# A hybrid decoder layer: the input projection with tokens kept on chip and weights streamed, in matmuls of 416 columns

## The chip, the cores and the metric

The kernel runs on one core of one Trainium2 chip. The metric is the device time of one launch in microseconds (us). The core has five engines that run side by side: TensorE (PE in the profile; PEld is its weight load), VectorE (DVE), ScalarE (ACT), GpSimd (POOL) and SyncE (SP). Here SyncE issues most transfers (its queue is SPq), GpSimd some stores, ScalarE a few loads. Matmuls read on-chip memory (SBUF) and write to PSUM, eight banks of 512 float32 columns in each of 128 partitions.

## The reference, cut to what matters

One layer for 4096 prompt tokens and 64 sample tokens, 4160 in all, with model width 1024:

```python
h = _rmsnorm(x, g_pre)
z = h @ w_in                      # 1024 -> 2816 columns
cb, cc, ch, cg, q, k, v, ag, mq, mg = _split_cols(z)
u = cc * ch                       # gated convolution over 3 tokens
conv = conv_w[0] * up[:, 0:t] + conv_w[1] * up[:, 1:t + 1] + conv_w[2] * up[:, 2:t + 2]
out_a = jax.nn.silu(cg) * cb * conv
out_b = jax.nn.silu(ag) * o_b     # o_b: attention in a window of 128 keys
out_c = jax.nn.silu(mg) * o_c     # o_c: attention over 256 memory tokens
y = jnp.concatenate([out_a, out_b, out_c], axis=-1) @ w_out
return x + _rmsnorm(y, g_post), new_conv, new_k, new_v
```

The change concerns `z = h @ w_in`: 4160 tokens, 22 column tiles of 128, 1024 values to sum over.

## The kernel before, in words

**Precision.** A float32 number is split into a high part (rounded to the format that TensorE multiplies) and a low part (the rest). A product of two split operands takes three matmuls per 128 values summed over: high x high, high x low, low x high. A split is a copy on ScalarE and a subtraction on VectorE: lines 183 and 187 for weights, 359 and 360 for tokens.

**Seven products for eight.** Two column tiles make a *pair*, two halves of the 1024 inputs make the rows, two half blocks of tokens make the columns: a 2 x 2 by 2 x 2 block product. Strassen's scheme in Winograd's form computes it with seven products in place of eight, from sums S1 to S4 of the weight blocks A11 to A22 and sums T1 to T4 of the token blocks B11 to B22 (`PRODUCTS`, line 40). Each product is four slices of 128 inputs x three matmuls = 12 matmuls (`product`, line 364, the matmul in line 369) of `HW` = 260 columns. `evict` (line 372) adds what a product left in PSUM to z tiles in SBUF: line 376 on VectorE, line 378 on ScalarE.

**Loops.** The 11 pairs are in three phases (`PHASES`, line 43) of 4, 4 and 3 pairs. In a phase the weights stay split on chip, and the eight blocks of 2 x 260 tokens pass by: for each phase, for each block, for each of the seven products, for each pair. Phase 0 scales the tokens by the gain and the row factor, and writes them to DRAM (`hd`), the sums T1 to T4 are written in phase 1, and later phases read them again. The first two blocks of phase 0 multiply plainly (eight products), before row factors are there, and scale z afterwards (`z_rows`, line 621). Sums of weights for a later phase are made during the phase before it and go through DRAM (`w_sums`, line 196).

**Ends.** What a column tile becomes follows in `finish` (line 486): a gate with a tanh (`finish_gate`, lines 429 and 430), a split q or k (`finish_parts`, lines 410 and 412), v (`finish_v`), or the convolution (`finish_conv`). The results go to DRAM (`md`, `qd`, `vd`) and are read by the attention.

**Order.** In phase 0 every engine runs in the order in which the code issues its instructions (`in_order`); in phases 1 and 2 a planner orders them, but for some that are held in program order. Phase 2 also computes keys and values of the memory tokens (`mem_acc`, line 794) and the attention of chunk 0, the first 256 of the prompt tokens. After the projection, `open_attention` (line 1010) opens the attention's buffers; there the 15 other chunks run between the matmuls of the output projection (line 1482).

Of the kernel before, what the change touches and what calls it, by code (L numbers as in the profile page):

```python
# [23 lines left out]
HW = 260  # L24
NBLK = NT // (2 * HW)
# [7 lines left out]

PRODUCTS = (("A11", "B11"), ("A12", "B21"), ("S2", "T2"), ("S3", "T3"), ("S1", "T1"), ("S4", "B22"), ("A22", "T4"))  # L40
NP_ = len(PRODUCTS)

PHASES = (((8, 9), (14, 15), (16, 17), (12, 13)), ((0, 1), (2, 3), (4, 5), (6, 7)), ((10, 11), (18, 19), (20, 21)))
PLAIN_BLOCKS = 2
# [7 lines left out]
def hybrid_layer(ctx: ExitStack, tc: tile.TileContext, a: dict):  # L52
# [6 lines left out]

# [4 lines left out]
    ones = const.tile([P, P], F32, name="ones")  # L64
    G.memset(ones, 1.0)
# [3 lines left out]
    convw = const.tile([P, 2, 3], F32, name="convw")  # L69

    zs = const.tile([P, 14, NS], F32, name="zs")

    diag = const.tile([P, 2 * HW], F32, name="mix_s")
    mix_s = diag[:, : 8 * NS].rearrange("p (k n) -> p k n", n=NS)

    rowd = [tc.dram_tile([2 * HW], F32, name=f"rowd{b}") for b in range(NBLK)]
    hd = [{o: tc.dram_tile([P, KH, HW], F32, name=f"hd{b}_{o}") for o in ("B12", *(o for _, o in PRODUCTS))}
          for b in range(NBLK)]
    sd = {}
    qd = tc.dram_tile([2, 7, P, NT], F32R, name="qd")  # L80
    vd = tc.dram_tile([P, NT], F32, name="vd")
    md = tc.dram_tile([KT, P, NT], F32, name="md")

    wa = ctx.enter_context(tc.tile_pool(name="wa", bufs=3 * NP_))
    pa = ExitStack()
    wb_stack = ExitStack()
    wb = wb_stack.enter_context(tc.tile_pool(name="wb", bufs=NP_, side="right"))  # L90
    psa = ExitStack()

    place = ctx.enter_context(tc.tile_pool(name="place", bufs=1)).tile([P, 2, KH, HW], F32, name="place")
    hxp = pa.enter_context(tc.tile_pool(name="hx", bufs=4))
    hp = pa.enter_context(tc.tile_pool(name="hp", bufs=2))
    own = ExitStack()
    kept_z = ExitStack()
    zp, used = {}, {1: [], 2: []}

    def z_pool(where, name, w=2):  # L100
        return where.enter_context(tc.tile_pool(name=name, bufs=1))

    def open_phase(ph):
        nonlocal tp, natp, pa2, pa1

        if ph == 0:
            z = [z_pool(kept_z, f"z{n}") for n in range(4)]
            natp = own.enter_context(tc.tile_pool(name="nat", bufs=2))
            zp[2] = [*z, z_pool(own, "z4")]
            kept_z.z4 = zp[2][-1]  # L110
        elif ph == 1:
            zp[2].remove(kept_z.z4)
            zp[2][:0] = [z_pool(own, f"z{n}") for n in (5, 6, 7)]
        else:

            tp = [own.enter_context(tc.tile_pool(name=f"t2{n}", bufs=3)) for n in "ab"]
            z = [z_pool(own, n) for n in ("z8", "z9", "y0", "y1", "z10", "y2")]
            zp[2], zp[1] = [z[0], z[1], z[4]], [z[2], z[3], z[5]]
        if ph < 2:
            tp = own.enter_context(tc.tile_pool(name=f"t{ph}", bufs=(7, 9)[ph]))  # L120
        if ph != 1:

            psa.close()
            bank = lambda name, bufs: psa.enter_context(tc.tile_pool(name=name, bufs=bufs, space=bass.MemoryType.PSUM))
            if ph == 0:

                pa2 = {tag: bank(f"pa{tag}", 2) for tag in "xy"}
            else:

                pa1 = {(tag, w): bank(f"p{tag}{w}", 1) for tag, w in (("x", 2), ("x", 1), ("y", 1), ("y", 2))}  # L130
                third["ps"] = bank("psm", 2)

    tp = natp = pa2 = pa1 = None

    def accumulator(i, w, name):
# [20 lines left out]
    def flush():  # L156
        for fn in late:
            fn()
# [1512 lines left out]
```

## Time and profile before

| what | before |
|---|---|
| median of 3 runs | 1543.01 us (1542.81 to 1544.86) |
| the profiled execution: its span from first to last instruction | 1539.4 us |
| granted TensorE clock, mean over the span | 0.999 |
| TensorE matmul, busy | 1529.5 us |
| VectorE, busy | 1146.7 us |
| ScalarE, busy | 806.7 us |
| GpSimd, busy | 380.7 us |
| moved by DMA | 305.59 MB, mean 199 GB/s |

The profiled execution's own launch time isn't listed apart from the runs; its span lies 3.6 us under their median, which is what lies around a span. A row of the windows reads: stretch in us from the span's start, its length, busy us of PE, PEld, DVE, ACT and POOL (each with its count of instructions), granted clock, share of time that the 16 DMA engines were busy, GB/s moved. A row of the chain reads: start, duration, engine, tile and line, count. A row of the timeline reads: start, duration, engine, line, operation, output and inputs with shapes, count, and in brackets the idle time before it with what ended it. A row of the groups reads: line, engine, operation, output and inputs, shapes, count, then busy us, mean ns of one, and the idle time of the engine just before them with what ended most of it. Matmuls are pipelined, so the duration of one matmul (0.28 us) is longer than the distance between two.

### The profile page before, as it was taken

The numbers are of one execution on the slowest core, as the hardware profiler recorded it, in microseconds if no ns is written. First come the engines' busy times: TensorE is split into PE (matmuls) and PEld (weight loads), VectorE is DVE, ScalarE is ACT, GpSimd is POOL, SyncE is SP. The second block draws the span as 40 slices with busy tenths as digits, with TensorE's granted clock in tenths as the row PEclk, the third lists the DMA queues.
The fourth block names the chain that finished last, engine by engine and source line by source line (L and its number), as shares of the span: only waits on it lengthen the run. The fifth ranks groups of instructions, "written<-read, shape, count | busy, mean of one in ns | idle before, by whom it ended". The sixth has DMA issues, their size and how long they took to land.

```text
span 1539.4 us, 30166 instructions
## 1 busy us (share of the span) xinstructions
PE 1529.5 (99%) x11341; PEld 1407.9 (91%) x11341; DVE 1146.7 (74%) x2059; ACT 806.7 (52%) x2047; POOL 380.7 (25%) x603
## 2 busy tenths in 40 slices
PE   9999999999999999999999999999999999999998
PEld 9999999999999999999999998788888888888876
DVE  6789888899888777897777769766666666666643
ACT  6686666476222222354454437765566556555632
POOL 0223332221400000000101203644444444444310
PEclk9999999999999999999999999999999999999999
DMA  9989999878755333677876789977777777777332
GB/s 261 180 239 252 271 272 263 276 241 288 193 180 180 126 126 126 214 223 280 223 258 236 217 295 266 228 165 148 161 148 148 151 156 153 157 160 150 124 110 96
DMA packets 175110, 305.59 MB, mean 199 GB/s; under 512 B 31093, under 2 KB 104821, under 8 KB 174933
## 3 DMA queue, kind: packets, MB, share of 16 engines
q1 hardware_dynamic: 128069, 226.69, 47.5%
q0 software_dynamic: 46176, 75.92, 24.7%
q8 instruction: 90, 1.47, 0.4%
q10 hardware_dynamic: 720, 1.05, 0.2%
q14 instruction: 55, 0.45, 0.1%
HBM read 196.54 MB, written 108.05 MB: 198 GB/s over the span
## 4 chain that ended last, share of the span: by engine, by line
PE 94%; DVE 2%; DMA 1%; ACT 1%; POOL 1%; issue 0%; ACTq 0%; SPq 0%; DVEq 0%; POOLq 0%
PE c L369 55%; PE y L1482 23%; PE ws L1250 4%; PE wo L1092 2%; PE wt L1273 2%; PE xs L1186 2%; PE xt L1201 2%; PE wo L1222 2%; PE wo L1228 1%; PE mem_acc L794 1%; DMA qd<-z 1%; DMA ws20A<-in_w_in 0%; POOL xp L1195 0%; DVE z L376 0%; DVE z L625 0%
## 5 line engine op out<-in xcount | busy, mean ns | idle before, releaser
L1482 PE MATMUL y<-wo,mh 128*128 128x512 f32 (+1 forms) x1040 | 350.1, 399 | 0.0
L376 DVE TENSOR_TENSOR z<-c,z 128x520 f32<-128x520 f32 (+1 forms) x308 | 195.3, 647 | 99.0 <-PE c L369 96.7
L1482 PEld LDWEIGHTS y<-wo,mh 128*128 128x128 f32 x1040 | 194.3, 188 | 39.3 <-issue 2.4
L1482 PE MATMUL y<-wo,ml 128*128 128x512 f32 (+1 forms) x520 | 201.8, 388 | 0.0
L1263 ACT ACTIVATE sm<-sm,wnm 128x128 f32<-128x128 f32 x256 | 99.6, 390 | 61.6 <-DVE wnm L1257 60.3
L1195 POOL TENSOR_SCALAR xp<-xp,xrd 128x256 f32<-128x256 f32 x128 | 76.9, 608 | 200.3 <-DVE xrd L1191 200.1
L1482 PEld LDWEIGHTS y<-wo,ml 128*128 128x128 f32 x520 | 98.2, 189 | 16.2
L1187 DVE TENSOR_REDUCE xmx<-xs 128x2 f32<-128x512 f32 x64 | 44.1, 689 | 58.2 <-PE xs L1186 58.1
L1275 ACT COPY wpt<-wt 128x512 f32<-128x512 f32 x64 | 37.2, 582 | 85.8 <-PE wt L1273 85.7
L1250 PEld LDWEIGHTS ws<-kst,q 128*128 128x128 f32 x512 | 70.0, 190 | 5.2 <-ACT xp L1190 0.5
L1489 DVE TENSOR_TENSOR yn<-y,gpost 128x512 f32<-128x512 f32 (+1 forms) x66 | 45.1, 683 | 39.6 <-PE y L1482 39.3
L1250 PE MATMUL ws<-kst,q 128*128 128x256 f32 x512 | 73.1, 283 | 0.1
L1490 ACT ACTIVATE y<-y 128x512 f32<-128x512 f32 (+1 forms) x66 | 38.6, 584 | 64.5 <-DVE yn L1489 64.5
L742 POOL CAST wmask<-negs 128x256 uint8<-128x256 f32 x1 | 0.8, 841 | 268.5 <-DMA negs<-in_wmask 268.5
L1190 ACT ACTIVATE xp<-xs,xnm 128x256 f32<-128x256 f32 x128 | 58.9, 464 | 7.0 <-DVE xnm L1188 6.7
L1283 POOL TENSOR_SCALAR_AFFINE_SELECT wpt<-wpt 128x512 f32<-128x512 f32 x64 | 51.2, 800 | 43.6 <-ACT wpt L1275 40.6
L1125 POOL DMA_DIRECT2D q<-qd x64 | 42.8, 674 | 71.5 <-DVE wo L187 61.1
L1280 POOL TENSOR_SCALAR_AFFINE_SELECT wpv<-wpt 128x512 f32<-128x512 f32 x62 | 40.4, 652 | 59.7 <-ACT wpt L1275 59.5
L1253 DVE COPY_PREDICATED sm<-wmask,ws 128x256 f32<-128x256 uint8 x124 | 52.2, 436 | 3.0 <-ACT sm L1252 2.8
L1114 POOL DMA_DIRECT2D kst<-qd x64 | 38.6, 617 | 63.8 <-PE xt L1201 41.5
L1500 DVE SCALAR_TENSOR_TENSOR xr<-yn,yst,xr 128x1024 f32<-128x1024 f32 (+2 forms) x34 | 43.1, 1269 | 14.1 <-POOL yst L1496 13.4
L378 ACT COPY z<-c 128x520 f32<-128x520 f32 (+1 forms) x44 | 24.4, 554 | 52.8 <-PE c L369 49.9
(962 smaller groups left out, 5135.6 us busy)
## 6 DMA issues: line engine op xcount, KB each, us to landing
q<-qd POOLq DMA_DIRECT2D x64, 384.0 KB, 8.0
xr<-in_x_p SPq DMA_DIRECT2D x32, 512.0 KB
nat<-in_x_p SPq DMA_DIRECT2D x39, 416.0 KB
o_yp<-xr SPq DMA_DIRECT2D x31, 512.0 KB
md<-th POOLq DMA_DIRECT2D x48, 260.0 KB, 6.4
qd<-zh SPq DMA_DIRECT2D x48, 260.0 KB
qd<-z SPq DMA_DIRECT2D x48, 260.0 KB
kst<-qd POOLq DMA_DIRECT2D x60, 192.0 KB, 5.7
```

Source lines behind the costliest of these rows:

```text
L369: TE.matmul(bank[:, :HW], l, r, start=first and i == 0, stop=last and i == 3 * KH - 1)
L376: add = lambda dst, other: V.tensor_tensor(dst, c, other, op=ALU.add)
L1187: V.tensor_reduce(mx[:, :nb], s, axis=AX.X, op=ALU.max)
L1190: S.activation(p[:, i, :], s[:, i, :], AF.Exp, bias=nm[:, i : i + 1], scale=SCALE, accum_out=den[:, i : i + 1])
L1195: G.tensor_scalar(p[:, i, :], p[:, i, :], rd[:, i : i + 1], 0.5, op0=ALU.mult, op1=ALU.mult)
L1250: TE.matmul(s3[:, hh, :], self.q[:, 4 + 2 * (2 * half + hh) + kvh, i * P : i * P + P], self.kst[:, 2 * kvh + part, i * P : i * P + 2 * P], ...
L1253: V.copy_predicated(sm[:, 2 * half : 2 * half + 2, :], third["wmask"], third["negs"] if first else s3[:, :, 0:P])
L1263: S.activation(sm[:, hh, :], sm[:, hh, :], AF.Exp, bias=nm[:, hh : hh + 1], scale=SCALE, accum_out=den[:, hh : hh + 1])
L1283: G.affine_select(p3, p3, pattern=[[0, 4], [1, P]], compare_op=ALU.is_ge, fill=0.0, base=0, channel_multiplier=-1)
L1482: TE.matmul(acc, self.hl[l][:, k], wo[k][c0 // 512][:, r, c0 % 512 : c0 % 512 + c1 - c0], start=j == 0, stop=j == passes * KT - 1)
L1489: V.tensor_tensor(yn[:m, c0:c1], acc[:m], gpost[:m, c0:c1], op=ALU.mult)
L1500: V.scalar_tensor_tensor(self.xr[:m, cs], yn[:m, cs], st[:m, 3:4], self.xr[:m, cs], op0=ALU.mult, op1=ALU.add)
```

## The change

- `HW` is 416: five blocks of 2 x 416 tokens. A block's seven split token operands lie in seven places in SBUF (`slot`), and the weights of all 11 pairs pass by: for each block, for each of six groups of pairs (five of two pairs, one of one pair), for each product, for each pair of the group. Tokens are read once from the input; `hd` and `sd` are gone.
- In block 0 and in the first group of block 1, weights are loaded raw, summed (S1 and S3 on GpSimd, S2 and S4 on VectorE) and split, and the split sums are stored in DRAM (`wd`). From there on split sums are loaded from `wd`, and A11, A12 and A22 are loaded raw and split again for every block.
- The products come in another order. Products 1 and 3, 2, 4 and 6, and 5 and 7 share a PSUM accumulator each ("AYAYZYZ"): a later product adds to what is there, and each state is read out by one VectorE addition or ScalarE copy.
- Only group 0 of block 0 multiplies plainly. In block 0 all z tiles are scaled by the row factors after the products (`z_rows`); in later blocks the tokens are scaled (`x_scale`).
- Every engine runs in written order to the end of the projection. A step is one product of one group; what happens in which step is set out in `plan_weights`, `plan_tokens`, `plan_ends`, `plan_start` and `plan_third`. In `step`, loads are issued first, then the first pair's product, half of the jobs, the second pair's product, the other jobs, and the eviction.
- Chunk 0 and the memory keys run in the last block. The output weights lie in the token operands' place.

The diff, cut to its core:

```diff
-HW = 260
-NBLK = NT // (2 * HW)
+HW = 416
+BW = 2 * HW
+NBLK = NT // BW
...
-PRODUCTS = (("A11", "B11"), ("A12", "B21"), ("S2", "T2"), ("S3", "T3"), ("S1", "T1"), ("S4", "B22"), ("A22", "T4"))
+PRODUCTS = (("A11", "B11"), ("S2", "T2"), ("A12", "B21"), ("S3", "T3"), ("S1", "T1"), ("A22", "T4"), ("S4", "B22"))
...
-PHASES = (((8, 9), (14, 15), (16, 17), (12, 13)), ((0, 1), (2, 3), (4, 5), (6, 7)), ((10, 11), (18, 19), (20, 21)))
-PLAIN_BLOCKS = 2
+PLAIN = (("A21", "B11"), ("A11", "B11"), ("A21", "B12"), ("A11", "B12"), ("A22", "B21"), ("A12", "B21"), ("A22", "B22"), ("A12", "B22"))
+
+GROUPS = (((14, 15), (16, 17)), ((0, 1), (2, 3)), ((4, 5), (6, 7)), ((18, 19), (20, 21)), ((12, 13),), ((8, 9), (10, 11)))
...
+    x1 = pool(ctx, "x1").tile([P, 6 * XS], F32R, name="x1")
+    x6 = pool(x2, "x2").tile([P, XS], F32R, name="x2")
+    zp = [pool(own, f"z{n}") for n in range(3)]
+    wp = [pool(own, f"w{n}") for n in range(5)]
...
+    wp.append(pool(early, "w5"))
...
+    def load_split(key):
+        b, g, q, o = key
+        w = ws[key] = w_of().tile([P, 2, 512], F32R, tag="w", name="w{}_{}_{}{}".format(*key))
+        DMA.dma_start(f(w), wd[GROUPS[g][q], o])
...
+    def fill_sum(key):
+        b, g, q, o = key
+        w = split_w(key, raws[key] if o == "S2" else raws.pop(key))
+        t = wd[GROUPS[g][q], o] = tc.dram_tile([P, 2, 512], F32, name=f"wd{g}_{q}{o}")
+        store(t, f(w))
+
+    def sums(b, g, q):
+        r = {o: raws.pop((b, g, q, o)) for o in ("A11", "A21", "A22")}
+        G.tensor_tensor(r["A22"], r["A21"], r["A22"], op=ALU.add)
+        G.tensor_tensor(r["A21"], r["A11"], r["A21"], op=ALU.subtract)
+        V.tensor_tensor(r["A11"], r["A22"], r["A11"], op=ALU.subtract)
...
+    def x_scale(b, o):
+        x, half = xs[b, o], int(o[2]) - 1
         for k in range(KH):
+            V.scalar_tensor_tensor(x[:, k], x[:, k], gain_of(o, k), rows[b][:, half * HW : (half + 1) * HW], op0=ALU.mult, op1=ALU.mult)
...
+    def z_rows(b, z):
+        z = z.rearrange("p a b n -> p a (b n)")
+        w = z.shape[1]
+        V.tensor_tensor(z, z, rows[b].unsqueeze(1).to_broadcast([P, w, BW]), op=ALU.mult)
...
+                if b == 0 or (b, g) == (1, 0):
+                    for t, o in ((s0 - 5, "A11"), (s0 - 4, "A21"), (s0 - 3, "A22"), (s0 - 2, "A12")):
+                        load_at(t, lambda o=o, b=b, g=g, qs=qs: [load_raw((b, g, q, o), o) for q in qs])
+                    key = lambda o, b=b, g=g, qs=qs: [(b, g, q, o) for q in qs]
+                    job_at(s0 - 2, *(lambda k=k: split_keep(k) for k in key("A11")))
+                    job_at(s0 - 1, *(lambda b=b, g=g, q=q: sums(b, g, q) for q in qs))
+                    job_at(s0 - 1, *(lambda k=k: fill_sum(k) for k in key("S2")))
+                    job_at(s0, *(lambda k=k: split_keep(k) for k in key("A12")), *(lambda b=b, g=g, q=q: last_sum(b, g, q) for q in qs))
+                    load_at(s0 + 1, lambda b=b, g=g, qs=qs: [load_raw((b, g, q, "A22"), "A22") for q in qs])
+                    job_at(s0 + 1, *(lambda k=k: fill_sum(k) for k in key("S3")))
+                    job_at(s0 + 2, *(lambda k=k: fill_sum(k) for k in key("S1")))
+                    job_at(s0 + 3, *(lambda k=k: fill(k) for k in key("A22")))
+                    job_at(s0 + 4, *(lambda k=k: fill_sum(k) for k in key("S4")))
+                else:
+                    for p, (o, _) in enumerate(PRODUCTS):
+                        u = s0 + p
+                        keys = [(b, g, q, o) for q in qs]
+                        if o[0] == "S":
+                            load_at(u - 2, lambda keys=keys: [load_split(k) for k in keys])
+                        else:
+                            load_at(u - 4, lambda keys=keys, o=o: [load_raw(k, o) for k in keys])
+                            job_at(u - 2, *(lambda k=k: fill(k) for k in keys))
...
+            for i, o in enumerate(("B11", "B12", "B22", "B21")):
+                load_at(s(3, 1 + i), lambda b=b, o=o: x_load(b, o))
+            for t, o in ((s(3, 6), "B11"), (s(4, 1), "B12"), (s(4, 3), "B22"), (s(4, 5), "B21")):
+                job_at(t, lambda b=b, o=o: x_scale(b, o))
+            sums_ = {(5, 0): "T1", (5, 1): "T3", (5, 3): "T2", (5, 5): "T4"}
+            for (g, p), o in sums_.items():
+                job_at(s(g, p), lambda b=b, o=o: x_sum(b, o))
+            for t, o in ((s(5, 2), "B11"), (s(5, 4), "T2"), (s(5, 4), "B21"), (s(5, 6), "T3"),
+                         (at[b, 0, 0], "T1"), (at[b, 0, 1], "T4"), (at[b, 0, 2], "B22")):
+                job_at(t, lambda b=b, o=o: x_split(b, o))
...
+        job_at(5, tsum("T1"))
+        job_at(6, tsum("T3"))
+        job_at(7, tsum("T2"), split("T2"))
+        job_at(8, split("T3"))
+        job_at(9, split("T1"), tsum("T4"))
+        job_at(10, split("T4"))
...
+                elif (b, g) == (0, 0):
+                    front_at(n, *scale(1), *done(1))
+                    front_at(n + 1, *scale(0), *done(0))
+                else:
+                    front_at(n - 1, *scale(1), *done(1))
+                    front_at(n, *scale(0), *done(0))
...
+        jobs = [*first.pop(i, ()), *jobs_at.pop(i, ())]
+        half = (len(jobs) + 1) // 2
...
+            (wo_, xo), c, begin, end = PRODUCTS[p], "AYAYZYZ"[p], p in (0, 1, 4), True
+        if begin:
+            zs_of.setdefault("acc", {})[c] = accumulator(f"c{b}_{g}_{p}")
+        acc = zs_of["acc"][c]
+        for q in qs:
+            product(ws[b, g, q, wo_], slot(3) if plain and xo == "B12" else operand[xo], acc[:, q], begin, end, not (plain or begin))
+            if q == 0:
+                for fn in jobs[:half]:
+                    fn()
...
+        for fn in jobs[half:]:
+            fn()
...
+            evict(p, acc, *zs_of[b, g])
```

In the prediction a group's *first eviction* in a bank that is used again is that of product 2 (S2 x T2), whose accumulator product 4 adds to; a *pair* is one pair of column tiles; *parts* are the splits of q and k.

1021 lines of the change are left out of this document (374 added, 647 removed).

## The prediction

> **What bounds the kernel now.** I read the page first (busy shares), then the table of windows, then the chain that ended last, in order of time.
>
> ```profile
> span 1539.4 us, 30166 instructions
> PE 1529.5 (99%) x11341; PEld 1407.9 (91%) x11341; DVE 1146.7 (74%) x2059; ACT 806.7 (52%) x2047; POOL 380.7 (25%) x603
> ...
> 600.00:640.00 40.00, 40.00 (x336) 40.00 (x336) 30.91 (x42) 12.78 (x17) 0.00 (x0) 1.00 0.43 153
> 690.00:700.00 10.00, 10.00 (x86) 10.00 (x85) 8.08 (x12) 5.80 (x12) 0.00 (x0) 1.00 1.02 354
> ...
> 5.67 0.39 PE L369 MATMUL c<-hi_0B,w_0A 128*128 128x260 f32 x1 [0.25 <-ACT w_0A L183]
> ...
> 112.75 239.31 PE c L369 x1992
> 710.00 1.37 PE mem_acc L794 x6
> 937.44 6.83 PE y L1482 x30
> 1001.50 2.77 PE y L1482 x12
> 1038.27 2.77 PE y L1482 x12
> ```
>
> TensorE is the bound: the chain runs through L369 for 239 us at a stretch, and the granted clock is 1.00. In steady flow 336 matmuls of 260 columns take 40 us, **119 ns** each; a matmul of 512 columns takes 1.37/6 = **228.3 ns**. Busy PE is no measure of waiting, so I count. The projection runs from 5.67 to 937.44 = 931.8 us. It holds (2 plain blocks x 32 + 6 x 28 + 8 x 28 + 8 x 21) products x 12 = 7488 matmuls x 0.119 = 891.1; 48 memory matmuls x 0.2283 = 11.0; and chunk 0 of the attention, 14.9 (a chunk's period, 1038.27 - 1001.50 = 36.8, less its 96 output matmuls x 0.2283). What is left, **14.8 us**, is all that TensorE waits there.
>
> **The change: the matmuls.** After it there are 2 x 8 + (5 x 11 - 2) x 7 = 387 products x 12 = 4644 matmuls of 416 columns. Columns hardly fall: 7488 x 260 = 1.947 million, 4644 x 416 = 1.932. What can be won is the part of a matmul's time that isn't columns. No row has 416: in proportion to 260 it would be 190.4 ns, in proportion to 512 185.5; on the line between the two rows 119 + 156/252 x 109.3 = **186.7**, taken since 416 lies between. 4644 x 0.1867 = 867.0, so -24.1 us (-6.9 to -29.6). [...] A step (one product, two weight pairs, 24 matmuls) becomes 4.48 us, with one pair 2.24.
>
> **VectorE: what it now does, and when.** All five engines' work in the projection is now in written order. In every step the eviction of the product stands behind all the step's other jobs on VectorE, and the product two steps later adds to or overwrites the same PSUM bank: an eviction that is late by over one step stops TensorE.
>
> ```profile
> L376 DVE TENSOR_TENSOR z<-c,z 128x520 f32<-128x520 f32 (+1 forms) x308 | 195.3, 647 | 99.0 <-PE c L369 96.7 <-DMA qd<-zh 1.6
> 13.90 1.68 DVE L590 SCALAR_TENSOR_TENSOR lo_0B<-x_0B,gpre,hi_0B 128x260 fp32r<-128x260 f32 x4
> 15.50 0.69 DVE L187 TENSOR_TENSOR w_0A<-wr_0A,w_0A 128x512 fp32r<-128x512 f32 x1
> 16.10 0.69 DVE L187 TENSOR_TENSOR w_1A<-wr_1A,w_1A 128x512 fp32r<-128x512 f32 x1
> ...
> 101.56 1.23 DVE L349 TENSOR_TENSOR x_2T<-place,x_2B 128x1040 f32<-128x1040 f32 x1
> 102.71 2.39 DVE L625 TENSOR_TENSOR z<-z,rb 128x1040 f32<-128x1040 f32 x2
> ...
> L359 ACT CAST hi_3T<-x_3T 128x1040 fp32r<-128x1040 f32 x8 | 8.5, 1062 | 8.0 <-PE c L369 4.8 <-DMA x_3T<-hd_T 3.2
> L429 ACT ACTIVATE th<-z 128x520 f32<-128x520 f32 x48 | 28.7, 634 | 16.2 <-DMA md<-th 11.8 <-DVE w_2A L187 1.8 <-DVE z L625 1.3
> ```
>
> In a queue a 512-element operation starts 0.60 after the last, one of 1040 1.15 after: 1.04 ns an element and 0.07. So 416 elements cost 0.5, 832 (gate, part, eviction) 0.93, 1664 (an x sum, an x split, a z scaling) 1.8; an x scaling, four of 416, 2.3 (from 1.68 for four of 260). ScalarE: 1.5 for a 1664 cast, 0.9 for 832.
>
> A steady group (blocks 1 to 4) needs 3 x 1.2 weight splits + 5 x 0.9 evictions + some 4 to 6 of gates and parts: under half of its 31.4 us. **Block 0 and the first group of block 1** also do, per group, 4 x 1.2 more splits and 4 x 0.6 of weight sums on VectorE (7.2), and in block 0 two z scalings (3.6), on top of the next block's token work (scalings 9.2, sums 7.2, splits 12.6). I set VectorE's queue against TensorE's steps, place by place, counting from the start of the plain products as if nothing waited there (they end at 8 x 4.48 = 35.8):
> - Group 1. In the last plain step T2's sum, cast and split end at 35.6, since ScalarE's cast stands behind an eviction. Behind them: S2's sums and splits 2.5, a z scaling 1.8, two gates that each wait for a tanh 3.1, T3's split 2.0, A12's splits 1.2, S4's sums 1.2: 47.4. Then a scaling 1.8, gates 3.0, T1's split 2.1, T4's sum 1.8, S3's splits 1.2, and only then the second product's eviction: 58.2. TensorE has done three products by 35.8 + 13.4 = 49.2 and needs that bank: **wait 9**.
> - Groups 2 and 3 (convolution): some 29 of 31.4 us, bunched at the seam: **1.5** together.
> - The last step of group 3 and group 4 (one pair, steps of 2.24). Step 7 of group 3 has 9.0 (eviction, scaling, two parts, sum, split, token scaling, eviction), group 4's steps 4.9, 3.4, 0.6, 3.4, 1.1, 4.0 and 3.8: 30 us of work in 4.5 + 15.7 of TensorE. Waits: 3.4 for S2, behind the parts and GpSimd; 6.2 for A12, behind scaling and parts; 1.9 for the first eviction: **11.5**.
> - Group 5: steps of 6.1, 3.9, 3.0, 3.9, 5.7, 3.9 and 8.8, so 35 in 31.4. Waits: 3.5 for S2, which GpSimd's four sums hold, 3.0 for the first eviction: **6.5**.
> - Seam to block 1: 8.8 and 7.9 in two steps of 4.48, with tanh and GpSimd to wait for: 4.8 for S2, 4.2 for A12, 3.0 for the eviction: **12**.
>
> Together **40**. The floor, where the work alone exceeds TensorE's time, is 2 (group 1: 33 in 31.4) + 10 + 4 = 16.
>
> **GpSimd.** It now makes S1's and S3's sums, 512 elements with two inputs, a form that no row has.
>
> ```profile
> L1283 POOL TENSOR_SCALAR_AFFINE_SELECT wpt<-wpt 128x512 f32<-128x512 f32 x64 | 51.2, 800 | 43.6 <-ACT wpt L1275 40.6
> L458 POOL TENSOR_TENSOR us<-z,z 128x64 f32<-128x64 f32 x2 | 7.1, 3568 | 31.0 <-DVE z L376 31.0
> L483 POOL TENSOR_TENSOR mix_s<-cacc,z 128x64 f32<-128x64 f32 x2 | 0.9, 462 | 0.2
> L1268 DVE TENSOR_TENSOR sm<-sm,wrd 128x512 f32<-128x512 f32 x64 | 44.0, 688 | 1.1
> L165 POOL DMA_DIRECT2D md<-th x48 | 26.2, 547 | 66.6 <-DVE th L430 44.4 <-DVE zs L432 19.1 <-DVE place L349 2.0
> ```
>
> Bounds 0.46 and 3.57; I take 1.0, near the 512-element row. VectorE waits for ten of them in groups 4, 5 and the seam, 10 x (0.46 to 3.57) in place of 10, so the 40 lies between 35 and 66. Stores of stored sums queue on GpSimd too (0.55 each, 8 a group): some 13 of 31 us, no bound.
>
> **Transfers.** Gone: the h blocks' writing and rereading. Added: in blocks 1 to 4 weights stream again, per pair 3 x 0.26 + 4 x 0.52 = 2.9 MB. A block moves 31.7 weights + 6.8 tokens + 9.8 results = 48 MB in 172.5 us, 280 GB/s, against 354 sustained above at no PE wait. Two steps of lead (8.96) cover 1.05 MB at 330 (3.2), what stands ahead on SyncE's queue and a landing; in group 4 the lead is 4.5. Cost 0 to 20, I take **4**.
>
> **Start, steady blocks, end.**
>
> ```profile
> 10.00:20.00 10.00, 10.00 (x84) 10.00 (x85) 7.28 (x13) 6.47 (x13) 0.00 (x0) 1.00 1.02 297
> 160.00:200.00 40.00, 40.00 (x336) 40.00 (x335) 33.25 (x40) 24.37 (x44) 12.66 (x20) 1.00 0.99 277
> 240.00:280.00 40.00, 40.00 (x335) 40.00 (x335) 32.92 (x41) 22.64 (x39) 12.64 (x20) 1.00 0.96 265
> 13.16 1.72 ACT L589 ACTIVATE hi_0B<-x_0B,gpre 128x260 fp32r<-128x260 f32 x4
> ...
> L277 ACT ACTIVATE nat<-nat 104x1024 f32<-104x1024 f32 x40 | 42.1, 1054 | 7.4 <-DMA nat<-in_x_p 7.4
> L277 ACT ACTIVATION_READ_ACCUMULATOR nat<-nat 104x1 f32 x40 | 7.4, 186 | 0.0
> ```
>
> Before step 2, 2.75 MB must land (B11, A21, A11, B12): 9.3 us at 297 from 1 us on, then 2.2 for the gain (four of 260 take 1.72), 1.5 cast, 1.8 split: late by 2 against a step 2 that would start some 9 us after the first matmul at 6. ScalarE's three squares (1.05 + 0.19 each) then wait for four row loads that are queued ahead of A12, so B21's and B22's splits come 2 and 1 late: **5** (0 to 8). Steady group 4 has the token scaling and group 3's parts against steps of 2.24: 2 in each of blocks 1 to 3, **6**. Last block (buffers one fewer, chunk 0's pieces in order on every engine) and the handover, where the last eviction holds the first output product: **3** (0 to 8). From 937 on the work is the same.
>
> **Sum.** Waits 5 + 40 + 6 + 4 + 3 = 58 for 14.8: +43.2; matmuls -24.1; +19.1. The profiled span is 1539.4 us, and the median of the runs 1543.0 has 3.6 around it: **1543.0 + 19.1 = 1562**.
>
> **Rivals.**
> - *Faster: VectorE's queue lags, and TensorE waits only where the work itself is too much.* Place: the seams of block 0; price 16 for the 40, with start 4 and other waits 5: 25, 1543 - 24.1 - 14.8 + 25 = 1529. It decides below 36 of waits in all. For it: before, VectorE is busy 33 of 40 us with all 336 matmuls in place. Against: there VectorE stands idle before evictions for 97 us in all, waiting for TensorE, so they are not queued behind other work as the new ones are.
> - *Transfers bound blocks 1 to 3.* If the mix gets no more than the 265 to 277 GB/s seen at a share near 1.0, a block needs 48.3/0.265 = 182 us for 174.5: +23 for the 4: 1581. Against: 354.
> - *No gain in the matmul.* At 190.4 ns: +17.2, 1579.
> [...]
> - *It moves nothing*: waits of 36 to 42 balance the matmuls: 1543.
>
> **Chances.** Forecast 0.44, faster 0.27, nothing 0.06, transfers 0.11, matmul 0.07, lock 0.05. About 0.2% (3 us) is what can be told from no change: faster 0.27, same 0.06, slower 0.67. The low end, 1532, takes in about half of the faster rival (some 0.13 stays below it); the high end, 1594, takes in the transfers, the matmul and the lock one at a time, and most of GpSimd's upper bound (1562 + 26); some 0.06 stays above, where two of them meet. Cases of one sign hold two thirds, so the likeliest one's own range stands beside it: 1550 to 1575.
>
> **What would show it.** Right: matmul starts 187 ns apart; TensorE gaps on VectorE's evictions and splits between 35 and 260 us, 40 in all; later blocks near 174 us each. Wrong: block 0 without gaps (VectorE queued less than I add up), gaps on weight loads in blocks 1 to 4 (transfers), matmuls 190 apart, or GpSimd sums far from 1.0. The largest risk is the 40: it is added by hand from a queue's order.

## The result and the profile after

| | before | after |
|---|---|---|
| median of 4 runs each, on the same chip | 1543.2 us | 1682.61 us (1677.95 to 1687.96) |
| ratio, 95% interval | | 1.0902 [1.0877, 1.0927] |
| span of the profiled execution | 1539.4 us | 1679.3 us |
| granted TensorE clock, mean over the span | 0.999 | 0.967 |

The forecast was 1562 in a range from 1532 to 1594. The direction came out, the size did not: the loss is 139 us where 19 were forecast.

First the head of the page of the changed kernel, with the slices of TensorE's busy time and of the granted clock:

```profile
span 1679.3 us, 23937 instructions
...
PE 1552.4 (92%) x8489; PEld 1403.4 (84%) x8489; DVE 1012.0 (60%) x1743; ACT 729.4 (43%) x1864; POOL 428.8 (26%) x667
...
PE   8799587997999989998998988799999999999998
...
PEclk9899798999999999998999999899999999999999
```

Before, both were at 9 throughout the projection. Here TensorE has holes, and so has the clock, the deepest of them in the first seven slices (to 294 us), where weights are summed for the first time. The windows put numbers to it. They are cut at the last evictions of block 1's first group (the last one with weight sums), of blocks 1, 2 and 3, and of the projection; the last two rows are stretches of steady flow:

```profile
8.20:300.50 292.30, 235.76 (x1123) 224.17 (x1124) 204.94 (x230) 126.06 (x195) 95.36 (x113) 0.90 0.68 221
300.50:458.00 157.50, 147.65 (x767) 144.11 (x766) 84.98 (x101) 49.09 (x72) 12.61 (x21) 0.99 0.85 262
458.00:643.00 185.00, 177.15 (x928) 174.65 (x928) 103.10 (x119) 62.60 (x87) 15.29 (x26) 0.99 0.85 265
643.00:829.00 186.00, 176.13 (x908) 173.18 (x906) 103.47 (x119) 61.60 (x87) 15.28 (x26) 0.97 0.84 262
829.00:1066.40 237.40, 211.77 (x1086) 198.97 (x1086) 120.12 (x185) 86.72 (x179) 38.94 (x66) 0.94 0.77 230
...
480.00:520.00 40.00, 40.00 (x214) 39.70 (x213) 15.22 (x20) 8.69 (x13) 2.16 (x4) 1.00 0.68 225
302.00:362.00 60.00, 60.00 (x320) 59.53 (x319) 24.38 (x31) 16.71 (x28) 1.62 (x3) 1.00 0.81 240
```

The whole projection before, from its first to its last matmul, in the same view:

```profile
5.67:937.44 931.77, 930.26 (x7667) 922.80 (x7668) 748.79 (x1065) 465.73 (x803) 128.54 (x190) 1.00 0.74 225
```

Length less the PE column is TensorE's idle time: 56.5 us, then 9.9, 7.9 and 9.9, then 25.6, together 110; before, it came to 1.5 us. The clock column adds a second loss: in windows of 1 us, busy time x (1 - granted clock), summed, gives 19.5 us to 300.5, 7.9 in what follows of blocks 1 to 3 and 8.7 in block 4: **36 us** lost while TensorE was busy at half speed; before, 0.0. The rows of steady flow show what went right. A row also counts the matmuls that lie across its edges, and in the difference of two rows they cancel: 320 - 214 = 106 matmuls in 20 us, 188.7 ns each. Before, by the two rows that the prediction shows, it was 336 - 86 = 250 in 30 us, 120.0 ns.

What ended TensorE's waits, up to 1110 us (columns: engine and line, what it waited for, us in total, times, longest):

```profile
PE c L603 <- DMA w_0S<-wd_0S: 28.6, 8, 5.0
PE c L603 <- ACT w_0S L140: 24.2, 4, 14.6
PE c L603 <- ACT z L612: 18.9, 7, 5.0
PE c L603 <- DVE z L610: 18.8, 9, 8.4
PE vtp L903 <- DMA vT<-vd: 9.4, 1, 9.4
```

Three kinds: stored weight sums that land late (w_0S from wd, all behind 370 us), weights that are split late (ACT w_0S, all in block 0 and the first group of block 1), and evictions on ScalarE (L612) and VectorE (L610) that stand behind other work. The longest wait and what follows it, from the timeline of TensorE:

```profile
170.82 2.43 PE L603 MATMUL c<-x,w_0A 128*128 128x416 f32 x12
187.79 4.56 PE L603 MATMUL c<-x,w_0S 128*128 128x416 f32 x12 [14.55 <-ACT w_0S L140]
196.60 3.95 PE L603 MATMUL c<-x,w_0A 128*128 128x416 f32 x12 [4.25 <-ACT z L612]
```

Twelve matmuls take 4.56 us behind the wait, where twelve in flow take 2.43 from first start to last end: half speed. Now what SyncE did ahead of that wait (timeline of SyncE's queue; duration is the time that issuing took):

```profile
155.85 6.01 SPq L189 DMA_DIRECT2D x1B<-in_xt  x2
161.96 1.92 SPq L148 DMA_DIRECT2D wr_0A<-in_w_in  x1
172.40 0.34 SPq L255 DMA_DIRECT2D rb<-rowd  x1
172.79 6.24 SPq L189 DMA_DIRECT2D x1B<-in_xt  x2
179.13 3.23 SPq L148 DMA_DIRECT2D wr_0A<-in_w_in  x3
...
381.95 2.23 SPq L153 DMA_DIRECT2D w_0S<-wd_0S  x1
384.28 0.38 SPq L153 DMA_DIRECT2D w_1S<-wd_1S  x1
394.93 0.32 SPq L255 DMA_DIRECT2D rb<-rowd  x1
395.34 0.94 SPq L189 DMA_DIRECT2D x2B<-in_xt  x2
...
397.31 1.45 SPq L153 DMA_DIRECT2D w_0S<-wd_0S  x2
```

Line 255 spreads the row factors of the next block over the partitions. It stands in SyncE's queue from 163.9 on and is issued at 172.40, and from 384.7 on and is issued at 394.93, since it reads what GpSimd writes, and that write takes long. Behind it stand weights of group 4. Its waits are 29.5 us in blocks 1 to 3:

```profile
SPq L255 <- DMA rowd<-r: 29.5, 3, 10.2
```

The write itself, from the view of the transfers from 150 to 180 us (columns: count, size, us from issue to landing):

```profile
rowd<-r POOLq DMA_DIRECT2D x1, 3.2 KB, 15.4
```

3.2 KB take 15.4 us. The write was issued at 157.0, and it doesn't suffer alone: from some 6 us after its issue all transfers crawl. Block 1's write, issued at 381.3, shows it too (windows of the changed kernel; the last two columns are the DMA engines' busy share and GB/s):

```profile
381.00:386.00 5.00, 5.00 (x29) 4.96 (x28) 1.36 (x2) 0.00 (x0) 1.03 (x2) 1.00 1.08 365
387.00:393.00 6.00, 5.72 (x31) 5.33 (x29) 1.02 (x1) 0.00 (x0) 0.00 (x0) 1.00 1.26 74
```

The engines stay busy and move a fifth. The other three writes behind the start do the same: 411 GB/s from 157 to 162 us and 91 from 164 to 170, 373 and then 118 in block 2, 374 and then 110 in block 3. So the spread isn't the only link between the write and TensorE's waits. The stored sum that TensorE waits for until 397.74 was issued at 381.95, ahead of the spread, and landed some 16 us later:

```profile
397.74 2.76 PE L603 MATMUL c<-x,w_0S 128*128 128x416 f32 x7 [5.02 <-DMA w_0S<-wd_0S]
```

Of the six waits on stored sums in blocks 1 to 3, three (10.8 us) are on such loads, and three (11.6 us) on loads that were issued behind the spread.

### The profile page after: what moved, and what is told of

It reads as the page before. It is cut to its first block, busy times and chain, and to the rows that moved or that the text cites. A ratio compares the mean times of both kernels' runs of the same rounds, so it can differ in the third digit from the quotient of the medians.

```text
span 1679.3 us, 23937 instructions
## 1 busy us (share of the span) xinstructions
PE 1552.4 (92%) x8489; PEld 1403.4 (84%) x8489; DVE 1012.0 (60%) x1743; ACT 729.4 (43%) x1864; POOL 428.8 (26%) x667
## 4 chain that ended last, share of the span: by engine, by line
PE 44%; issue 2%; DMA 2%; DVE 1%; ACT 1%; POOL 0%; SPq 0%; DVEq 0%; POOLq 0%; ACTq 0%
PE y L1235 21%; PE c L603 8%; PE ws L1003 3%; PE wo L845 2%; PE wt L1026 2%; PE xs L939 2%; PE xt L954 2%; PE wo L975 2%; PE wo L981 1%; DMA vT<-vd 1%; PE mem_acc L517 1%; DMA gpost<-in_gpost 0%; DMA kst<-qd 0%; DMA qd<-zh 0%; DVE z L610 0%
## 5 line engine op out<-in xcount | busy, mean ns | idle before, releaser
L603 PE MATMUL c<-x,w_0S 128*128 128x416 f32 x1392 | 303.9, 370 | 73.3 <-DMA w_0S<-wd_0S 28.6
L1235 PE MATMUL y<-x 128*128 128x512 f32 (+1 forms) x1296 | 369.0, 399 | 0.0
L603 PEld LDWEIGHTS c<-x,w_0S 128*128 128x128 f32 x1392 | 274.4, 200 | 87.2 <-ACT w_0S L140 34.7
L1235 PEld LDWEIGHTS y<-x 128*128 128x128 f32 x1296 | 238.2, 189 | 46.1 <-issue 1.6
L603 PE MATMUL c<-x,w_0A 128*128 128x416 f32 x1140 | 241.4, 362 | 26.7 <-ACT z L612 18.9
L603 PEld LDWEIGHTS c<-x,w_0A 128*128 128x128 f32 x1140 | 219.6, 195 | 35.1 <-ACT z L612 21.4
L610 DVE TENSOR_TENSOR z<-c,z 128x832 f32<-128x832 f32 (+1 forms) x145 | 137.2, 946 | 164.7 <-PE c L603 158.9
L603 PE MATMUL c<-x,w_1S 128*128 128x416 f32 x1152 | 236.4, 354 | 0.0
L603 PEld LDWEIGHTS c<-x,w_1S 128*128 128x128 f32 x1152 | 218.8, 191 | 2.8 <-issue 0.4
L603 PE MATMUL c<-x,w_1A 128*128 128x416 f32 x960 | 196.4, 354 | 0.0
L603 PEld LDWEIGHTS c<-x,w_1A 128*128 128x128 f32 x960 | 180.9, 190 | 2.8 <-issue 1.2
```

Source lines behind the costliest of these rows:

```text
L603: TE.matmul(bank[:, :HW], l, r, start=first and i == 0, stop=last and i == 3 * KH - 1, skip_group_check=more)
L610: add = lambda dst, other: V.tensor_tensor(dst, c, other, op=ALU.add)
L1235: TE.matmul(acc, self.hl[l][:, k], wo[k][c0 // 512][:, r, c0 % 512 : c0 % 512 + c1 - c0], start=j == 0, stop=j == passes * KT - 1)
```

## The experiments

Theories. **A**: SyncE's queue is held by the spread. **B**: the queue of VectorE (with GpSimd's sums) in block 0, as the prediction had it, only more of it. **C**: the rate of the transfers. **D**: VectorE and GpSimd hold each other up. **E**: the clock falls behind waits. **F** and **G**: the written order of VectorE's jobs, or their amount. In the table, "against after" is the median less 1682.61; the kernel before, timed anew beside each of the five sets of runs, stood at 1540.8 to 1543.2, so differences between sets are good to some 2 us beside the intervals. gap_short and gap_long have two runs each, the others four.

| run | median us | ratio to before, 95% interval | against after |
|---|---|---|---|
| rows_early | 1662.97 | 1.079 [1.077, 1.0809] | -19.6 |
| sums_on_dve | 1673.47 | 1.0854 [1.0831, 1.0877] | -9.1 |
| no_z_scaling | 1660.38 | 1.0785 [1.0741, 1.0828] | -22.2 |
| clock_filler | 1686.72 | 1.0937 [1.0921, 1.0953] | +4.1 |
| gap_short | 1709.19 | 1.1086 [1.1064, 1.1108] | +26.6 |
| gap_long | 1759.89 | 1.1415 [1.1392, 1.1438] | +77.3 |
| values_early | 1666.12 | 1.0784 [1.0746, 1.0823] | -16.5 |
| block0_light | 1620.53 | 1.052 [1.0488, 1.0551] | -62.1 |
| three_together | 1645.37 | 1.0672 [1.0641, 1.0703] | -37.2 |
| evict_first | 1673.18 | 1.0843 [1.0824, 1.0861] | -9.4 |
| end_queues | 1677.31 | 1.0876 [1.086, 1.0892] | -5.3 |
| four_together | 1639.21 | 1.0627 [1.0604, 1.0649] | -43.4 |

### rows_early: the row factors ten steps sooner

```diff
-                t = s(2, 0) + i
+                t = s(1, 4) + i
-            job_at(s(3, 2), lambda b=b: row_factors(b))
+            job_at(s(2, 6), lambda b=b: row_factors(b))
```

> One edit: the row loads and squares of the next block's tokens, and the row factors that GpSimd makes of them, come ten steps earlier; the spread of the factors stays at its step. Nothing is left out. Theory A (SyncE's queue is held: the spread at line 255 waits on SyncE until the factors are written, and the weights of group 4 and the stored sums stand behind it): the 14.5 us wait on w_0S at 173 us goes, as do the waits of 3 to 5 us on w_0S in the middle of blocks 1 to 3, and the slow stretches behind them; 35 to 55 us less than the changed kernel, 1628 to 1648. Theory B (VectorE's queue in block 0 sets the waits): these waits come back as waits on VectorE's evictions and splits, within 8 us of 1682.6. Theory C (the rate of the transfers itself bounds): the same bytes at the same times, no change.

TensorE's waits on stored sums between 300 and 840 us, in the changed kernel and then in rows_early:

```profile
PE c L603 <- DMA w_0S<-wd_0S: 22.5, 6, 5.0
```

```profile
PE c L603 <- DMA w_0S<-wd_0S: 3.5, 2, 2.3
```

The gain is about half of what theory A forecast. In blocks 1 to 3 the waits go as it has it: 19 us of waiting on w_0S go, the waits on evictions rise from 4.8 to 10.0, and with the clock 18.3 us are gained from the cut at block 1 to the end of block 3. But the edit moves the write itself, and the crawl of the transfers moves with it, ahead of the steps that load group 4 (rows_early; block 1's write was issued at 359.8):

```profile
363.00:369.00 6.00, 6.00 (x34) 5.95 (x33) 5.11 (x6) 1.74 (x2) 0.55 (x1) 1.00 0.70 44
376.00:382.00 6.00, 3.68 (x14) 3.24 (x13) 1.58 (x2) 0.00 (x0) 0.00 (x0) 0.79 1.08 369
```

So the write of the row factors is shown as the source of these waits. How much of it acts through SyncE's queue and how much through the slow transfers is not shown: the spread alone was not moved to another queue. In block 0 theory A does not hold: the 14.5 us wait at 173 us goes, but group 1 of block 1 begins only 4.3 us sooner (last eviction ahead of it at 296.2 instead of 300.5). The timelines of rows_early say what took its place: the spread is issued at 170.18, at once, but the token loads around it take 1.3 to 3.3 us each to issue and the three raw weights behind them 6.65, while the DMA engines show a busy share of 0.91 to 1.12 and 280 to 422 GB/s in every us from 164 to 181, which speaks for full transfer engines (theory C, in this one place, argued and not tried), and three new or longer waits stand in those groups, 2.98 and 2.12 us on VectorE's evictions and 4.25 on a split.

### sums_on_dve: the weight sums off GpSimd

```diff
-        G.tensor_tensor(r["A22"], r["A21"], r["A22"], op=ALU.add)
-        G.tensor_tensor(r["A21"], r["A11"], r["A21"], op=ALU.subtract)
+        V.tensor_tensor(r["A22"], r["A21"], r["A22"], op=ALU.add)
+        V.tensor_tensor(r["A21"], r["A11"], r["A21"], op=ALU.subtract)
```

> One edit: the two sums that GpSimd makes of each weight pair (S1's and S3's, 22 in all that take 1.26 to 2.82 us there) are made on VectorE, 0.6 to 0.7 each, 14 us of VectorE's time in block 0 and the seam. Nothing is left out. Theory B (VectorE's queue sets the waits): 8 to 15 us more than the changed kernel, 1690 to 1698. Theory D (the two engines hold each other up: VectorE's two-input operations take 1.77 instead of 0.68 beside such a sum, and VectorE's third sum waits for GpSimd's): 5 to 15 us less, 1668 to 1678, and no VectorE operation of 512 elements over 1.0 us at the sums.

VectorE gets 15 us more work (22 operations of 0.69) and the kernel is 9 us faster: theory D, though the edit takes away two things at once, the hold-up and GpSimd's slower sums. Groups of VectorE up to 300 us, S2's sum with the sums on GpSimd (the changed kernel), then with them on VectorE (columns: busy us, mean ns, idle before it):

```profile
L168 DVE TENSOR_TENSOR wr_0A<-wr_0A,wr_0A 128x512 f32<-128x512 f32 x6 | 7.3, 1215 | 21.8 <-POOL wr_0A L167 21.8
```

```profile
L168 DVE TENSOR_TENSOR wr_0A<-wr_0A,wr_0A 128x512 f32<-128x512 f32 x6 | 4.2, 692 | 0.2
```

VectorE waited 21.8 us for GpSimd, and beside it the operation took 1215 ns in the mean instead of 692. The hold-up in both directions, from the changed kernel's timelines of VectorE and of GpSimd:

```profile
130.19 1.77 DVE L141 TENSOR_TENSOR w_1A<-wr_1A,w_1A 128x512 fp32r<-128x512 f32 x1
...
134.80 1.77 DVE L168 TENSOR_TENSOR wr_0A<-wr_0A,wr_0A 128x512 f32<-128x512 f32 x1
```

```profile
129.79 1.62 POOL L167 TENSOR_TENSOR wr_0A<-wr_0A,wr_0A 128x512 f32<-128x512 f32 x1
...
133.21 2.82 POOL L167 TENSOR_TENSOR wr_1A<-wr_1A,wr_1A 128x512 f32<-128x512 f32 x1
```

### no_z_scaling and block0_light: take work from block 0

no_z_scaling:

```diff
-                scale = lambda which: [... z_rows(b, z(which))] if b == 0 else []
+                scale = lambda which: [... z_rows(b, z(which))] if False else []
```

> One edit: block 0's results are not multiplied by their tokens' row factors, which is left out of the computation; it takes some 20 us from VectorE (eleven operations of 1.9 us or two of 0.9), all between 35 and 270 us. Theory B (VectorE's queue in block 0 sets the waits there): 20 to 35 us less than the changed kernel, 1648 to 1663, with the waits on VectorE's evictions nearly gone. Theory A (SyncE's queue): at most 10 us less, the 14.5 us wait at 173 us stands.

block0_light is rows_early with this edit and without the four sums of a weight pair in `sums` and `last_sum`:

> On top of the earlier row loads (rows_early, 1663): block 0's results are not multiplied by the row factors, and no sums of weight blocks are made (the raw blocks stand in their places, split and stored as before); both are left out of the computation. VectorE loses some 20 + 13 us of work before 270 us, GpSimd 28 and the waits for it. Theory B (the queues of VectorE and GpSimd in block 0 set its waits): 40 to 65 us less than rows_early, 1598 to 1623, block 0's groups 2, 3 and 5 at 32 to 35 us each. Rival (ScalarE's queue, transfers and the clock hold block 0 anyway): at most 25 less, 1638 or more.

Theory B's forecast of the time holds in both. 20 us of VectorE's work less give 22 us; VectorE's evictions still hold TensorE for 5.5 us up to 300 us (15.3 before the edit), and the 14.5 us wait stays (13.7 us ahead of 174.99), as theory A has it. block0_light is 42 us under rows_early (1662.97), and in the traces the last eviction of block 1's first group comes 40.6 sooner (255.6 for 296.2). Its waits up to 300 us (lines 600 and 607 there are 603 and 610 of the changed kernel):

```profile
PE c L600 <- DVE z L607: 10.9, 4, 5.1
PE c L600 <- ACT z L609: 9.8, 2, 8.9
PE c L600 <- ACT w_0A L140: 2.3, 1, 2.3
```

No wait on a split sum is among them. Up to that eviction the idle time is 23.3 us where rows_early has 49.3, and the clock's loss 10.2 where it has 20.1.

### clock_filler, gap_short, gap_long: what a wait costs beyond itself

clock_filler:

```diff
+        if (b, g, p) == (0, 4, 1):
+            for _ in range(60):
+                TE.matmul(acc[:, 1, :HW], operand["B11"][:, 0, 0, :P], operand["B11"][:, 0, 0], start=True, stop=True)
```

> One edit: 60 matmuls whose result nobody reads (11.2 us at full clock) stand ahead of the step that waits 14.5 us at 173 us, written into the unused half of its accumulator. Nothing is left out. Theory E (a wait of over some 3 us drops the granted clock, and the matmuls after it run at half speed for several us): the granted clock from 185 to 205 us is near 1.0 instead of 0.50 to 0.72, and the group ends 4 to 6 us earlier; 1676 to 1679 if nothing else waits. If the slow matmuls after the wait have another cause: no change of the clock there, time the same or up to 3 us more.

A miss. The threshold of some 3 us was the author's estimate: in the changed kernel's timeline up to 1110 us the 13 waits of 3.48 us and more all have a drop of the clock behind them, but the shortest wait with one is 2.35 us (52.80 to 55.15). The filler kept the clock at 1.00 up to 188 us, but 2.1 us of waiting were left behind it, and from some 188 to 191.6 the clock stood at 0.50 all the same: the drop came later, it did not go. So its price seemed to hang on there being a wait, not on the wait's length, and the next two runs measure that in places that had been free of waits:

```diff
+        if 0 < b < 4 and g < 3 and p in (2, 5):
+            o, last = operand[PRODUCTS[p][1]], zs_of["acc"]["AYAYZYZ"[p - 1]][:, 0, :8]
+            for k in (0,):
+                V.scalar_tensor_tensor(o[:, 0, k, :8], last, 0.0, f(o[:, 0, k, :8]), op0=ALU.mult, op1=ALU.add)
```

gap_long has `:HW` for `:8` and `(3, 2, 1, 0)` for `(0,)`.

> One edit: at 18 steps of blocks 1 to 3 (groups 0 to 2, the third and sixth product), in flow that had no wait, VectorE rewrites 8 columns of the product's operand with themselves plus 0 times the product before, so that TensorE must wait for that product's eviction (1.0 us) and this operation. Nothing is left out. 18 gaps of some 1.3 to 1.6 us: 23 to 29 us by themselves. Theory E (the granted clock falls only after a wait of over some 2 us, and then for 3 to 4 us whatever the wait's length): no drop, 23 to 30 us more than the changed kernel, 1706 to 1713. If every wait costs clock: 18 x 1.5 to 2 more, 1733 to 1750.

> The same 18 places; VectorE rewrites the whole high half of the operand with itself plus 0 times the product before (four operations of 416 columns, 0.5 to 0.6 each), the part that TensorE needs first last. Nothing is left out. 18 gaps of some 3.0 to 3.6 us: 54 to 65 us by themselves. Theory E: each is followed by 3 to 4 us at a granted clock of 0.50, 1.5 to 2 us each; 27 to 36 more, in all 81 to 101 us more than the changed kernel, 1764 to 1784. Without a cost of the clock: 1737 to 1748.

Both fell as theory E has it, gap_long 4 us under its band (at the first of the 18 places there was a wait already; 17 are clean). One gap of gap_short, with the granted clock in the column behind POOL's:

```profile
327.73 1.49 PE L603 MATMUL c<-x,w_1S 128*128 128x416 f32 x7
330.50 2.51 PE L603 MATMUL c<-x,w_0A 128*128 128x416 f32 x12 [1.28 <-DVE x L702]
```

```profile
329.00:334.00 5.00, 3.72 (x21) 3.50 (x20) 2.30 (x4) 0.62 (x1) 0.00 (x0) 1.00 0.03 11
```

Two gaps of gap_long, one with a drop and one without:

```profile
324.21 4.50 PE L603 MATMUL c<-x,w_0A 128*128 128x416 f32 x12 [3.27 <-DVE x L702]
...
385.82 2.52 PE L603 MATMUL c<-x,w_0A 128*128 128x416 f32 x12 [3.20 <-DVE x L702]
```

```profile
325.00:330.00 5.00, 5.00 (x16) 4.78 (x16) 0.00 (x0) 0.00 (x0) 0.00 (x0) 0.52 0.31 120
...
388.00:393.00 5.00, 5.00 (x28) 4.95 (x27) 1.02 (x1) 1.15 (x2) 0.00 (x0) 1.00 0.57 167
```

Of 15 inserted gaps of 1.28 to 1.71 us none dropped the clock; of 19 of 3.20 to 5.20 (2 in gap_short, 17 in gap_long) 14 did. In the blocks that hold them (from 287 us on, behind the first place) there are 5 drops in gap_short and 14 in gap_long, with those behind other waits, and the clock cost 9.5 and 30.7 us: **1.9 to 2.2 us each**. From 280 us to the end of block 3 gap_long has 31 us more of idle time and 22 more of the clock's loss than gap_short; the medians lie 50.7 apart.

### values_early and end_queues: the last block

values_early: `load_at(n0 + 12, first_chunk)` becomes `n0 + 10`.

> One edit: what chunk 0 of the attention loads in the last block (keys, values, mixing rows) is asked for two steps earlier. Nothing is left out. Theory (the 9.4 us wait for the values' load at 916 us is a wait on a load asked for one step ahead on SyncE's queue): the wait goes with the slow stretch behind it, 8 to 12 us less than the changed kernel, 1670 to 1675. Rival (SyncE's queue and the shrunken buffers hold the last block, so that the time comes back at the next load): within 4 us.

No wait of over 1 us for the values is left, and the group that had the wait takes 40.2 us from eviction to eviction for 47.7: 7.5 gained there. The median's gain is larger, but its runs lie 21 us apart (1655.70 to 1676.41), so only the 7.5 seen in its trace are put down to this edit.

end_queues:

```diff
-        DMA.dma_start(wo_raw[j], a["w_out"][k][:, 512 * h : 512 * h + 512])
+        G.dma_start(wo_raw[j], a["w_out"][k][:, 512 * h : 512 * h + 512])
-        DMA.dma_start(third["gpost"], a["gpost"].partition_broadcast(P))
+        S.dma_start(third["gpost"], a["gpost"].partition_broadcast(P))
```

> One edit at the end of the projection: the output weights' loads are issued from GpSimd's queue and the load of the last norm's gain from ScalarE's, both out of SyncE's queue. Nothing is left out. Theory A for the end (SyncE's queue, in which the output weights wait 17 us for buffers and the gain stands behind the last keys' load): the 4.7 us wait on w_0S at 1040 us and the 7.8 us of the gain's load in the chain go, 8 to 14 us less than the changed kernel, 1668 to 1675. Rival (buffers and the last results hold the handover, not the queue): within 4 us, or more where GpSimd's queue now holds its stores: up to 1695.

Nearer to its rival. The wait on w_0S went but for 0.6 us, and a longer one came at the same place, an eviction behind splits of output weights that now wait in GpSimd's queue; the gain's load is still in the chain that ended last. TensorE's waits from 1000 to 1090 us:

```profile
PE c L603 <- DVE z L610: 10.8, 1, 10.8
PE wt L1026 <- DVE sm L1021: 6.2, 1, 6.2
PE ws L1003 <- DVE z L610: 3.8, 1, 3.8
```

What bounds the handover stays open.

### three_together, evict_first, four_together: order and what adds up

> The edits of rows_early, sums_on_dve and values_early together: row loads and factors ten steps earlier, the weight sums on VectorE, chunk 0's loads two steps earlier. Nothing is left out. Each alone took some 20, 9 and 8 us off the changed kernel's 1682.6. If the three remove different waits they add up: 1643 to 1650. If they share a cause in block 0 (VectorE's queue takes back what SyncE's and GpSimd's give): 1655 to 1665.

They add up: -37.2, the sum of 19.6, 9.1 and some 8. That fits three edits that remove different waits; it rests on the 7.5 of values_early's trace, since with the 16.5 of its median the sum would be 45.

evict_first puts the second half of a step's jobs behind its eviction, in block 0 and group 0 of block 1:

```diff
+        late_jobs = not plain and (b == 0 or (b, g) == (1, 0))
-        for fn in jobs[half:]:
+        for fn in () if late_jobs else jobs[half:]:
             fn()
...
             evict(p, acc, *zs_of[b, g])
+        for fn in jobs[half:] if late_jobs else ():
+            fn()
```

> One edit: in block 0 and the first group of block 1 the second half of a step's jobs (splits, sums, scalings, gates on VectorE, ScalarE and GpSimd) is queued behind the step's eviction instead of ahead of it. Nothing is left out. Theory F (the written order makes the waits: evictions are late because other jobs stand ahead of them, the work itself would fit): the waits on evictions in block 0 go, 15 to 35 us less than the changed kernel, 1648 to 1668. Theory G (the amount of VectorE's work between the seams makes them): what the evictions gain the splits lose, within 8 us of 1682.6, or more if the splits now come too late: up to 1710.

Between the two: -9.4. TensorE's waits for evictions on both engines up to 300 us fall from 28.7 to 12.9 us, those for split weights rise from 29.0 to some 33. The order is a part of block 0's loss; the amount of work is the larger one, going by the 22 us of no_z_scaling and the 42 of block0_light.

> The three edits of three_together and that of evict_first. Nothing is left out. If the order's part of block 0's waits is separate from what the earlier rows and the sums on VectorE took: 1645.4 - 9.4 = 1636, 1633 to 1639. If the three had already removed it (evict_first's largest gain is the 7 us at the same wait at 173 us that rows_early takes away): 1642 to 1650. Over 1541.8 in either case: block 0's amount of work on VectorE and the clock's drops behind its waits stay.

1639.21, between the two forecasts: some 6 of evict_first's 9.4 us come on top, roughly, since its runs (1634.73 to 1644.48) and those of three_together (1641.92 to 1652.45) overlap. This is the fastest version that computes everything, and it is still 1.0627 times the kernel before. In its first 300 us:

```profile
8.00:300.00 292.00, 251.64 (x1217) 239.33 (x1218) 214.81 (x260) 132.19 (x204) 60.22 (x93) 0.92 0.71 238
```

40 us of idle time remain there, with VectorE busy 74%.

## Why the prediction was wrong, point by point

The step that failed is the sum of the waits. 58 us were added up, and 112.5 us of idle time came; each wait was priced as itself alone, and the clock's loss behind the waits, 36 us, was put at nothing.

- **The matmuls: the gain right, the time of one not.** 119 and 186.7 ns were taken, 120.0 and 188.7 are measured; the 119 came from a row whose 336 matmuls include some that lie across its edges, while the chain's own row (1992 in 239.31 us) has 120.1. 7488 x 0.1200 - 4644 x 0.1887 = 22.3 us were won for 24.1, because both times were too short, which is luck in part. The proportional rival's 190.4 is as near to 188.7 as the forecast's 186.7, but its gain of 6.9 us is out.
- **Block 0 and the start: right in mechanism, too small.** 45 were forecast (5 + 40), 59 of idle time came (56.5, and 2.5 more than before ahead of the first matmul). At the first place the queue was added up to 9 and 8.4 came. In group 4 the sum missed that raw weights wait in SyncE's queue, for the spread (issued at 172.40) and behind two token loads that took 6.24 us to issue (172.79) while 413 GB/s moved (175 to 180 us): one wait of 14.5. GpSimd's sum was taken at 1.0 us; alone it takes 1.26 (183.64), beside VectorE up to 2.83 (48.57).
- **VectorE and GpSimd holding each other up: given too little.** The chances give a lock between the two 0.05, and the high end of the range takes it in. No row of before shows one: the attention's two-input operation (L1268) has 688 ns in the mean, but only 6 of that row's 64 operations ran beside GpSimd work at all, of another form, and those 6 took 682 to 692 ns, no longer than the rest. What the runs showed in its place: beside GpSimd's sums of 512 elements VectorE's two-input operations of 512 take up to 1.79 us for 0.68 (43.86, changed kernel), and with the sums on VectorE the time is 9.1 us less. How much of the 9.1 is the hold-up and how much GpSimd's slower sums is not shown, as the edit takes both away.
- **The clock: not in the sum at all.** 36 us were lost. The row of before had a clock of 1.00, and its projection 1.5 us of idle time in all; the added waits should have carried a surcharge, some 2 us for each of the 20 drops that the changed kernel shows up to 1110 us.
- **Transfers and steady blocks: wrong cause.** 10 us were forecast (4 + 6), 27.6 idle came, 22.5 of them on stored sums. Not the sustained rate (262 to 265 GB/s moved, far under the 413 that the same trace shows at 175 to 180 us) but the write of the row factors: transfers crawl behind it (74 to 118 GB/s), and the spread at line 255 stands in SyncE's queue in the step in which the factors are still being written. The prediction listed what is queued behind a wait on VectorE and GpSimd, and on SyncE counted bytes alone, at a rate of 330 GB/s that was the author's estimate (329 moved from 630 to 640 us before, 354 from 690 to 700). rows_early moves the write and takes 19 of the 22.5 away; it doesn't separate the two links.
- **Last block and handover: 3 forecast, some 38 came** (25.6 idle, and the end of the kernel 12 us later behind the last eviction than before). Chunk 0's loads and the output weights share SyncE's queue with the stored sums. Shown for the values (7.5), not settled for the rest.
- **The 14.8 us "that TensorE waits" before: mostly no waits.** Worked out as a remainder, it was taken for waiting and subtracted as removable. The view shows 1.5 us of idle time. 7.5 are the one nanosecond by which each of the 7488 matmuls was taken too short; what the other 6 are stays open.

The sum with what was measured: -22.3 for the matmuls, +110 + 2.5 - 1.5 idle, +36 clock, +12 handover, some 3 unassigned: 140, the difference of the two spans. (What lies around a span is 1.8 us in the runs listed with both, 1681.09 against 1679.3, and not the 3.6 that the prediction took; the sum doesn't depend on it.)

## What to carry to other kernels

When a change gives up slack, price each new wait as itself plus what the clock takes behind it (here some 2 us for each drop), and write out every in-order queue, that of the transfers too: an instruction there that waits on a slow small write holds the loads of another group. Place such a write where no load is near its deadline, since here the transfers fell to 74 to 118 GB/s for 5 to 7 us behind it. A remainder of a sum is not a wait until a view shows idle time. And a first block that must make what later blocks reread has its own balance of engines; half of this loss is there (59 idle and 19.5 of clock), in a sixth of the time.

## What the runs showed of the hardware

- Behind 20 of the changed kernel's waits of TensorE up to 1110 us the granted clock fell to 0.50, some 2 to 5 us after the wait began, and returned 3 to 7 us after the matmuls resumed. In windows of 0.1 us, 12 of these low stretches last 3.4 to 3.5 us, six 6.8 to 6.9, one 10.2 and one 17.0: one, two, three and five times the shortest. The short ones cost 1.5 to 1.7 us of TensorE's time each, all 20 on average 2, after a wait of 2.4 us (110.43 to 112.82) as after one of 14.5. The shortest wait with a drop is 2.35 us (52.80 to 55.15), and in three_together 2.05 (ahead of 170.74); three of 2.89 to 2.98 (ahead of 409.21, 580.42 and 828.96) left the clock at 1.00. Inserted waits of up to 1.71 us in steady flow cost no clock (15 of 15), and of the 17 of 3.20 to 3.62 us five escaped too. What decides between equal waits is not shown.
- Two-input operations of 512 elements on VectorE and GpSimd slowed each other in the changed kernel: VectorE's splits and sums (lines 141 and 168) take 0.68 us alone (124.54) and up to 1.79 beside GpSimd's sums (43.86), GpSimd's sums (166 and 167) 1.26 alone (183.64) and up to 2.83 beside VectorE's operations (48.57).
- A write of 3.2 KB in single elements, issued from GpSimd, landed after 9.1 to 15.4 us in the changed kernel and after 8.2 to 9.8 in rows_early. Beginning some 6 us after each of the last four issues, the other transfers of the changed kernel fell for 5 to 7 us from 365 to 411 GB/s to 74 to 118, at a busy share of the DMA engines of 1.16 to 1.70; the kernel before has the same behind its writes (273 GB/s from 133 to 139 us, 98 from 142 to 147, for the write issued at 139.7). Why is not shown.
- Issuing held SyncE's queue: 3.0 us for one token load while some 410 GB/s moved (155.85), 0.8 at 365 (380.30), 0.47 at 131 (395.34).
